# One slab of its own for the sample's transposed probabilities, and smaller slabs beside it

## The chip, the cores and the metric

The kernel runs on one core of a Trainium2 chip. The metric is the time of one execution on the device in microseconds (us), lower is better. The engines of the core are TensorE (PE; its weight loads are shown as PEld), VectorE (DVE), ScalarE (ACT), GpSimd (POOL) and SyncE (SP), which issues nearly all loads. Each runs its instructions in the order of its own list and waits for the others by semaphores.

## What is computed

One inference step of a backbone of two layers over 384 tokens of width 1024: 128 prompt tokens and 256 sample tokens with a different conditioning. Cut to what matters here:

```
mod = silu(cond) @ w_mod + b_mod                 # six vectors a layer: sh1, sc1, g1, sh2, sc2, g2
h = rms_norm(x, norm1) * (1 + sc1) + sh1
proj = h @ w_in                                  # q, k, v, latents, hyena input, gates
o_a = softmax(q_a k_a^T) v_a                     # 8 heads; the sample also reads 128 cached keys
o_b = softmax(q_b k_b^T) v_b                     # 8 heads, keys and values from a latent
o_c = hyena(hy_in)                               # two long convolutions, filters made by a small net (hy_w1, hy_w2, hy_w3)
x = x + g1 * (sum_n sigmoid(gate_n) * (o_n @ w_branch_n)) @ w_out
h = rms_norm(x, norm2) * (1 + sc2) + sh2
x = x + g2 * (silu(g) * a) @ ffn_down            # a, g = split(dwconv3(h @ ffn_up))
```

All in float32. The sample's attention has 256 queries and 384 keys for each of 16 heads a layer.

## The kernel before

Tokens lie along the free dimension, channels along the 128 partitions. A float32 product is made of three products of rounded parts, hi with hi, hi with lo, lo with hi (`mm3`, L268 to L270; most of TensorE's time). The parts are made by `hi_lo`: a ScalarE copy to the rounded type (`copy_a`, L230) and a VectorE subtraction (L234). `tt` (L237) and `stt` (L240) are VectorE's other helpers, so one line of the profile stands for many places; tiles and shapes tell them apart.

**Space.** All passing buffers come from slabs. A `Slab` is a stretch of every partition, s0 with 1920 floats and s1 to s10 with 3072, and holds one type at a time, plain or rounded float32. `Arena.alloc` looks through the slabs in order and takes, of all places that are wide enough, the one that has been free for longest (a wholly empty slab counts as 10000 steps younger, so it is taken last). When an empty slab is taken for the other type, it becomes a new tile, and its first writer waits for every reader of the old one. So which slab a buffer gets decides what its writer must wait for.

**Order.** The program is written as generators that are woven together with given ratios (`weave`), and a scheduler sorts each engine's instructions by its estimate of when each can run, with the waits that the slabs bring. A buffer at another place gives another order on all engines, not just for its own instructions.

**The places that the steps touch.** The start: identity, the tables and weights of the filter net (`filters`, L480 and on: the pieces of `hy_w3` at L498, window and bias at L500 and L501), `w_mod` in eight loads (L369), the inputs, then the first two parts of `w_in` (L248), all on SP's one queue. The filter of the first layer is made in two halves of channels by `prep` (sums and differences of weights, L237 over 128x256, and their rounded parts, 128x512 and 64x512), `taps` (matmuls L551, times the window, L237 128x512), `sizes` (absolute values on ScalarE, L569, maxima on VectorE, L237 128x256) and `spectra` (column sums L586, L588 and L589, the spread factor L594, DFT matmuls L606 and their products, L237 128x512). Beside it `mod_vec` (L372 and on) makes the modulation: matmuls L378, a ScalarE copy, transposes L302, two additions L237 over 128x16, and for the scales L240 over 128x16, which writes `avs`. `norm_h` (L413 and on) then makes `h` in eight pieces: a product (L237 128x384), two ScalarE instructions with `avs` as scale (L436), and the parts of `h` (L443 and L237, or L230 and L234). With them the first projection starts.

The attention (`attention`, L960 and on) sweeps the heads: scores, softmax, then four stages later the transposes of the probabilities (`turned`, L302) and their copies to space. For each head of the sample `sample_turn` (L1031) takes a buffer of 3x256 floats, `pTs[h]`, at the first of its two query blocks; `outputs` multiplies it with the values (L1008) and frees it, four heads at a time.

Of the kernel before, what the change touches and what calls it, by code (L numbers as in the profile page):

```python
# [38 lines left out]
PS_FFN = {"mm": "0123", "fl": "456", "tr": "456"}  # L39
N_W = 4  # L40
N_BASE = 9728
SLABS = (1920, *[3072] * 10)
R_RE = 0.25
R_F0 = 3
U_CH, U_MLA = 20, 20
# [139 lines left out]
def kernel(  # L185
# [15 lines left out]
    split_slab = Slab(ctx, tc, 2 * N_W * 1024, "split")  # L201
    h_slab = Slab(ctx, tc, 2 * KD * T, "h")
    FA = Arena([Slab(ctx, tc, n, f"s{i}") for i, n in enumerate(SLABS)])
    RA = Rounded(FA)

    def banks(**lines):
# [22 lines left out]
    def copy_a(out, in_, scale=1.0):  # L229
        act.activation(out=out, in_=in_, func=AF.Copy, scale=scale)  # L230
# [74 lines left out]
    def add_sq(k, src, first):  # L305
        if first:
            sums.append(FA.alloc(T, top=True))
        acc = sums[0].ap()
# [20 lines left out]
    def load_vecs(l):  # L329
        st = FA.alloc(4, 128)  # L330
        s = [st.ap()[:, i] for i in range(4)]

        def rows(i, r0, n, src):
            sp.dma_start(out=s[i][r0:r0 + n, :], in_=src.rearrange("(r p) -> r p", p=128))

        for r0, n, src in ((0, 2, hy_freq[l]), (2, 1, hy_b1[l:l + 1]), (3, 1, hy_b2[l:l + 1])):
            sp.dma_start(
                out=s[3][r0:r0 + n].rearrange("r (h p) -> r h p", h=2),
                in_=src.unsqueeze(1).to_broadcast([n, 2, 64]),
            )  # L340
        pv = ps_of("tr", 4)
        transpose(pv, s[3][:4])
        dve.tensor_copy(out=vecs[l][:, 112:116], in_=pv)
        yield
        rows(0, 0, 48, b_mod[l])
        rows(0, 48, 8, norm1[l])
        rows(0, 56, 8, norm2[l])
        rows(0, 64, 36, hy_short_w[l].rearrange("i n -> (i n)"))
        rows(0, 100, 12, hy_short_b[l])
        pv = ps_of("tr", 112)  # L350
        transpose(pv, s[0][:112])
        dve.tensor_copy(out=vecs[l][:, 0:112], in_=pv)
        yield
        rows(1, 0, 88, ffn_conv_w[l, 0:2].rearrange("i n -> (i n)"))
        rows(2, 0, 44, ffn_conv_w[l, 2])
        rows(2, 44, 44, ffn_conv_b[l])
        pv = ps_of("tr", 176)
        transpose(pv[:, 0:88], s[1][:88])
        transpose(pv[:, 88:176], s[2][:88])
        dve.tensor_copy(out=vecs[l][:, 116:292], in_=pv)  # L360
        st.free()
# [45 lines left out]
    def sqrt_ahead(part):  # L407

        b = FA.alloc(1)
        act.activation(out=b.ap(), in_=part, func=AF.Sqrt)  # L410
        b.free()

    def norm_h(l, which):  # L413
# [3 lines left out]
        acc = sums.pop()  # L417
        st, dg = FA.alloc(4), FA.alloc(3, 128)
        sa = st.ap()[:, 0:3]
# [43 lines left out]
    def reduce_sin(l, dst, src, fr, b, n, np_):  # L463

        a = FA.alloc(n)
        q = FA.alloc(n)
# [207 lines left out]
    def hyena_open(y):  # L674
        y.oT = [RA.alloc(4, T, top=True) for _ in range(2)]
        y.db = [RA.alloc(12, 128, top=True) for _ in range(2)]
        y.dt = [b.ap() for b in y.db]
        st = FA.alloc(12, 128)
        sp.dma_start(out=st.ap(), in_=t_dft.rearrange("p (a b) -> p a b", b=128))
        hi_lo(y.dt[0], y.dt[1], st.ap())  # L680
        st.free()
# [43 lines left out]
    def hyena_chain(y, hf):  # L725

        R, dt, tok = RA, y.dt, y.tok[hf]
        A = slice(None)
# [231 lines left out]
    def attention(heads, q_of, kp_of, ks_of, vp_of, vs_of, scale, oT, pairs=False):  # L960

        jobs = []
        pts, pTs = {}, {}
# [17 lines left out]
        def turned(pa):  # L981
            n = pa.shape[1]
            pt = ps_of("at", n, 128)
            for u in range(n):
                transpose(pt[:, u], pa[:, u])
            return pt
# [44 lines left out]
        def sample_turn(hs, i, pb):  # L1031
            for u, h in enumerate(hs):
                pt = turned(pb.ap(len(hs), 3, 128)[:, u])
                if i == 1:
                    pTs[h] = FA.alloc(3, 256)
                copy_a(pTs[h].ap()[:, :, (i - 1) * 128:i * 128], pt)
            pb.free()

# [7 lines left out]
        for j in range(j0, j1):  # L1046
            two = (2 * j, 2 * j + 1)
            for hs in (two,) if pairs else (two[:1], two[1:]):
                for i in (1, 2):
                    jobs.append((lambda hs=hs, i=i: scores(hs, i, T), lambda pb, hs=hs, i=i: sample_turn(hs, i, pb)))  # L1050
            if (j - j0) % 2:
                jobs.append((None, lambda j=j: outputs(j - 1, j == j0 + 1)))
# [10 lines left out]
    def gqa(q, proj, oT):  # L1063
        qT, kT = q["qT"], q["kT"]
        vt = [q["vc"].ap(), proj[1][1].ap(), proj[2][1].ap()]
        yield from attention(
            list(range(8)),
            lambda h: qT.ap()[:, h],
            lambda h: [b.ap()[:, h // 4, 0:128] for b in kT],
            lambda h: [b.ap()[:, h // 4, 128:512] for b in kT],  # L1070
            lambda h: proj[0][1].ap()[:, 64 * (h // 4):64 * (h // 4) + 64],
            lambda h, n: vt[n][:, 64 * (h // 4):64 * (h // 4) + 64],
            64 ** -0.5, oT, pairs=True,
        )
        for b in (qT, *kT, q["vc"], *[pr[1] for pr in proj]):
            b.free()
# [295 lines left out]
    def urgent(line, by):  # L1372

        if by < 0:
            yield from line
            return
        while True:
            with tc.high_priority(offset=by):
                if next(line, line) is line:
                    return  # L1380
            yield
# [16 lines left out]
    def chain(*lines):  # L1398
        for g in lines:
            yield from g  # L1400
# [22 lines left out]
    vl = [load_vecs(l) for l in range(NL)]  # L1423
    fl = filters(0, RA, spec, True)
    next(fl)
# [37 lines left out]
    for l in range(NL):  # L1463
# [20 lines left out]
        g_ring = Ring(FA, 8, T, top=True)  # L1484
        oA = [RA.alloc(4, T, top=True) for _ in range(2)]
        oB = []
        att = chain(prep(l, proj, q := {}, RA), gqa(q, proj, oA), urgent(mla(l, q, proj, oB, RA), U_MLA))
        gs = []
# [133 lines left out]
```

## Time and profile before

| | us |
|---|---|
| median of 3 runs | 1530.76 |
| lowest, highest | 1525.3, 1531.33 |
| the profiled execution | 1531.72 |
| its span, first to last instruction | 1529.9 |
| TensorE busy in it | 1476.9 |
| VectorE busy | 1011.2 |
| ScalarE busy | 755.0 |

The profile is of one execution. Busy time is the time in which an engine had an instruction under way; a wait is put down to what ended it. Matmuls are pipelined: the time of one stands at twice its pitch in a full stretch, and the pitch of 128x384 is what such a stretch advances by. The granted clock is TensorE's share of 2.4 GHz: 1.00 is that, 0.50 is 1.2 GHz, values between are a mean over the window. A line of the profile names the program's line that issued it, and tiles without their numbers: `s` is any of the slabs, `base` holds weights as loaded and x, `split` the parts of weights, `h` the parts of the normed input, `banks` the PSUM banks.

### The profile page before, as it was taken

The numbers are of one execution on the slowest core, as the hardware profiler recorded it, in microseconds if no ns is written. First come the engines' busy times: TensorE is split into PE (matmuls) and PEld (weight loads), VectorE is DVE, ScalarE is ACT, GpSimd is POOL, SyncE is SP. The second block draws the span as 40 slices with busy tenths as digits, with TensorE's granted clock in tenths as the row PEclk, the third lists the DMA queues.
The fourth block names the chain that finished last, engine by engine and source line by source line (L and its number), as shares of the span: only waits on it lengthen the run. The fifth ranks groups of instructions, "written<-read, shape, count | busy, mean of one in ns | idle before, by whom it ended". The sixth has DMA issues, their size and how long they took to land.

```text
span 1529.9 us, 22305 instructions
## 1 busy us (share of the span) xinstructions
PE 1476.9 (97%) x8615; PEld 1355.3 (89%) x8615; DVE 1011.2 (66%) x1938; ACT 755.0 (49%) x1380; POOL 91.3 (6%) x120
## 2 busy tenths in 40 slices
PE   5899999999999999999999999999999999999997
PEld 2588889989889799999997887999898989999997
DVE  4756658646447796677767585785564767567674
ACT  2544347555454664444546444755455455344343
POOL 0112220000000000000000121100000000000000
PEclk9789999999999999999999999999999999999999
DMA  8714453425466433344355335342243524333531
GB/s 287 225 42 132 148 187 103 143 71 159 140 216 218 160 125 109 119 154 145 104 193 166 118 129 179 99 120 78 74 130 117 193 97 138 119 116 111 166 106 60
DMA packets 182448, 210.05 MB, mean 137 GB/s; under 512 B 25940, under 2 KB 166470, under 8 KB 182342
## 3 DMA queue, kind: packets, MB, share of 16 engines
q1 hardware_dynamic: 182342, 208.63, 42.9%
q8 instruction: 68, 1.11, 0.3%
q14 instruction: 38, 0.31, 0.1%
HBM read 206.48 MB, written 2.13 MB: 136 GB/s over the span
## 4 chain that ended last, share of the span: by engine, by line
PE 85%; DMA 6%; ACT 4%; DVE 3%; issue 1%; SPq 0%; POOL 0%; DVEq 0%; ACTq 0%
PE banks L268 25%; PE banks L270 24%; PE banks L269 24%; PE banks L302 3%; DMA base<-in_w_in_dram 3%; PE banks L976 2%; PE banks L378 2%; PE banks L1008 2%; DVE s L237 1%; DVE split L234 1%; ACT s L230 1%; ACT split L230 1%; DMA base<-in_w_mod_dram 1%; DMA s<-in_hy_w_dram 1%; DVE s L234 1%
## 5 line engine op out<-in xcount | busy, mean ns | idle before, releaser
L230 ACT ACTIVATE split<-base 128x1024 fp32r<-128x1024 f32 (+2 forms) x272 | 280.8, 1041 | 354.5 <-PE banks L269 260.9
L234 DVE TENSOR_TENSOR split<-base,split 128x1024 fp32r<-128x1024 f32 (+2 forms) x272 | 327.0, 1207 | 174.2 <-ACT split L230 171.0
L268 PE MATMUL banks<-h,split 128*128 128x384 f32 x1280 | 433.6, 342 | 4.5 <-DVE h L443 2.3
L270 PE MATMUL banks<-h,split 128*128 128x384 f32 x1280 | 434.7, 340 | 1.0 <-DVE split L234 1.0
L269 PE MATMUL banks<-h,split 128*128 128x384 f32 x1280 | 434.8, 340 | 0.3 <-DVE h L234 0.3
L268 PEld LDWEIGHTS banks<-h,split 128*128 128x128 f32 x1280 | 241.4, 189 | 17.8 <-issue 8.1
L269 PEld LDWEIGHTS banks<-h,split 128*128 128x128 f32 x1280 | 242.2, 189 | 4.5 <-DVE h L234 1.5
L270 PEld LDWEIGHTS banks<-h,split 128*128 128x128 f32 x1280 | 241.9, 189 | 3.4 <-DVE split L234 1.3
L269 PE MATMUL banks<-s,split 128*128 128x384 f32 x672 | 225.4, 337 | 0.0
L270 PE MATMUL banks<-s,split 128*128 128x384 f32 x672 | 225.3, 338 | 0.0
L268 PE MATMUL banks<-s,split 128*128 128x384 f32 x672 | 222.8, 338 | 0.0
L240 DVE SCALAR_TENSOR_TENSOR s<-banks,base,s 128x127 f32<-128x127 f32 (+1 forms) x448 | 172.5, 411 | 9.6 <-ACT s L457 5.5
L230 ACT ACTIVATE s<-banks 128x384 f32<-128x384 f32 (+9 forms) x260 | 114.4, 475 | 118.6 <-PE banks L302 53.2
L230 ACT ACTIVATE s<-s 128x384 fp32r<-128x384 f32 (+4 forms) x142 | 81.6, 580 | 109.9 <-DVE s L237 48.2
L268 PEld LDWEIGHTS banks<-s,split 128*128 128x128 f32 x672 | 125.7, 188 | 3.5 <-issue 1.1
L270 PEld LDWEIGHTS banks<-s,split 128*128 128x128 f32 x672 | 126.1, 188 | 1.7 <-DVE base L240 0.8
L269 PEld LDWEIGHTS banks<-s,split 128*128 128x128 f32 x672 | 126.1, 188 | 0.9 <-issue 0.2
L237 DVE TENSOR_TENSOR s<-banks,s 128x512 f32<-128x512 f32 (+3 forms) x132 | 81.7, 645 | 43.0 <-PE banks L270 21.9
L240 DVE SCALAR_TENSOR_TENSOR base<-banks,base 128x128 f32<-128x128 f32 (+1 forms) x128 | 46.9, 412 | 78.1 <-PE banks L270 78.1
L302 PE MATMUL banks<-base,s 128*128 128x128 f32 (+1 forms) x483 | 84.1, 282 | 8.7 <-DMA s<-in_hy_short_b_dram 2.0
L302 PEld LDWEIGHTS banks<-base,s 128*128 128x128 f32 (+1 forms) x483 | 61.5, 145 | 28.9 <-issue 7.1
L234 DVE TENSOR_TENSOR s<-s,s 128x384 fp32r<-128x384 f32 (+3 forms) x102 | 66.9, 660 | 18.5 <-ACT s L230 17.6
(147 smaller groups left out, 1741.7 us busy)
## 6 DMA issues: line engine op xcount, KB each, us to landing
base<-in_w_in_dram SPq DMA_DIRECT2D x40, 1024.0 KB
base<-in_ffn_up_dram SPq DMA_DIRECT2D x40, 1024.0 KB
base<-in_w_mod_dram SPq DMA_DIRECT2D x28, 1024.0 KB
s<-in_w_mod_dram SPq DMA_DIRECT2D x14, 1024.0 KB
base<-in_ffn_down_dram SPq DMA_DIRECT2D x16, 896.0 KB
base<-in_w_branch_dram SPq DMA_DIRECT2D x24, 512.0 KB
base<-in_w_out_dram SPq DMA_DIRECT2D x8, 1024.0 KB
base<-in_ffn_down_dram SPq DMA_DIRECT2D x8, 1024.0 KB
```

The costliest lines, as they stand in the source:

```text
L230: act.activation(out=out, in_=in_, func=AF.Copy, scale=scale)
L234: dve.tensor_tensor(out=lo, in0=src, in1=f(hi), op=ALU.subtract)
L237: dve.tensor_tensor(out=out, in0=a, in1=b, op=op)
L240: dve.scalar_tensor_tensor(out=out, in0=a, scalar=s, in1=b, op0=op0, op1=op1)
L268: pe.matmul(out, l[0], r[0], start=start, stop=False)
L269: pe.matmul(out, l[0], r[1], start=False, stop=False)
L270: pe.matmul(out, l[1], r[0], start=False, stop=stop)
L302: pe.transpose(out, in_, ident[:n, :n])
L378: pe.matmul(gv[32 * j:32 * j + 32], cT[:, 2 * k + j // 2], raw[:, j // 2, (j % 2) * 512:(j % 2) * 512 + 512], start=k == 0, stop=k == KD / ...
L976: pe.matmul(out, q_of(h)[:, i * 128:(i + 1) * 128], k, start=m == 0, stop=m == len(ks) - 1)
L1008: last = pe.matmul(p[b:b + 64, u], v, pT, start=start, stop=stop, tile_position=(0, b)).ins
```

## The change

The ordinary slabs become one of 1408 and nine of 3072 floats; a slab of 3584 floats, `extra`, stands beside them. The sum per partition is 32640 floats in both. A second arena, `XA`, has the extra slab first and the same ordinary slabs behind it; only the sample's `pTs[h]` are taken from it. The extra slab has room for four of them (768 floats each), later ones go where `Arena.alloc` finds the place that has been free longest, among all slabs.

```diff
--- before.py
+++ after.py
@@ -39,7 +39,8 @@
 PS_FFN = {"mm": "0123", "fl": "456", "tr": "456"}
 N_W = 4
 N_BASE = 9728
-SLABS = (1920, *[3072] * 10)
+SLABS = (1408, *[3072] * 9)
+N_EXTRA = 3584
 R_RE = 0.25
 R_F0 = 3
 U_CH, U_MLA = 20, 20
@@ -201,6 +202,7 @@
     split_slab = Slab(ctx, tc, 2 * N_W * 1024, "split")
     h_slab = Slab(ctx, tc, 2 * KD * T, "h")
     FA = Arena([Slab(ctx, tc, n, f"s{i}") for i, n in enumerate(SLABS)])
+    XA = Arena([Slab(ctx, tc, N_EXTRA, "extra"), *FA.slabs])
     RA = Rounded(FA)
 
     def banks(**lines):
@@ -1032,7 +1034,7 @@
             for u, h in enumerate(hs):
                 pt = turned(pb.ap(len(hs), 3, 128)[:, u])
                 if i == 1:
-                    pTs[h] = FA.alloc(3, 256)
+                    pTs[h] = XA.alloc(3, 256)
                 copy_a(pTs[h].ap()[:, :, (i - 1) * 128:i * 128], pt)
             pb.free()
```

No instruction is added, removed or changed; each engine's order is another one. Lines of the kernel after stand one (from L43) or two (from L204) further down. In the rows below, `s_1_112` and the like are slab tiles, `base_101` is the tile of `base`, `split_421` or `split_420` that of the weights' parts.

On SP, at the start, behind the first `w_mod` load. Before:

```order
L369 DMA base_101<-in_w_mod_dram 128x2x1024
L498 DMA s_1_112<-in_hy_w_dram 64x2x256
L500 DMA s_1_149<-in_t_win_dram 128x3x256
L501 DMA s_1_149<-in_hy_bias_dram 128x2x256
L525 DMA s_1_149<-in_t_kdft_dram 128x1280
L334 DMA s_1_113<-in_b_mod_dram 48x128
```

and after:

```order
L371 DMA base_101<-in_w_mod_dram 128x2x1024
L500 DMA s_1_149<-in_hy_w_dram 64x2x256 x2
L502 DMA s_1_149<-in_t_win_dram 128x3x256
L500 DMA s_1_149<-in_hy_w_dram 64x2x256 x2
L503 DMA s_1_149<-in_hy_bias_dram 128x2x256
L527 DMA s_1_156<-in_t_kdft_dram 128x1280
```

The three next loads of filter weights (hy_w), which stood ten rows further down behind the inputs' loads, now stand around the window table.

On VectorE, around the first modulation, before: the rows are the copy of vectors (L360), low parts of `w_in` (L234), the norm's small matrix (L425), modulation additions (128x16), filter work (128x512, 128x256, 64x512), the norm's first products (128x384), and last `avs` (L240).

```order
L360 COPY base_101<-banks 128x176
L234 TENSOR_TENSOR split_421<-base_101,split_421 128x1024
L425 TENSOR_SCALAR s_1_268<-base_101,s_1_268 128x128 x3
L237 TENSOR_TENSOR base_101<-banks,base_101 128x16
L234 TENSOR_TENSOR split_421<-base_101,split_421 128x1024
L237 TENSOR_TENSOR s_1_143<-s_1_112,s_1_143 64x512
L237 TENSOR_TENSOR base_101<-base_101,banks 128x16
L237 TENSOR_TENSOR s_1_200<-s_1_268 128x256
L237 TENSOR_TENSOR s_1_114<-banks,s_1_200 128x512 x3
L237 TENSOR_TENSOR s_1_108<-base_101,banks 128x384 x4
L237 TENSOR_TENSOR s_1_169<-banks,s_1_169 128x512
L240 SCALAR_TENSOR_TENSOR base_101<-base_101 128x16
```

After, up to `avs` again (L242 there, L236 for the low parts, L239 for L237):

```order
L239 TENSOR_TENSOR s_1_108<-base_101,banks 128x384 x3
L239 TENSOR_TENSOR s_1_149<-s_1_124 128x256
L239 TENSOR_TENSOR s_1_108<-base_101,banks 128x384
L239 TENSOR_TENSOR s_1_149<-s_1_124 128x256
L236 TENSOR_TENSOR split_420<-base_101,split_420 128x1024 x3
L239 TENSOR_TENSOR base_101<-banks,base_101 128x16
L236 TENSOR_TENSOR split_420<-base_101,split_420 128x1024
L362 COPY base_101<-banks 128x176
L239 TENSOR_TENSOR base_101<-base_101,banks 128x16
L239 TENSOR_TENSOR s_1_114<-banks,s_1_149 128x512 x3
L239 TENSOR_TENSOR s_1_112<-banks,s_1_156 128x512
L242 SCALAR_TENSOR_TENSOR base_101<-base_101 128x16
```

All four low parts of `w_in` and the three products of the filter's DFT (s_1_114) now stand in the twelve rows that end with `avs`; above these rows stand the tap products that came behind it.

On ScalarE, between the first layer's FFN and the second layer: rounded weights (128x1024), squares for the norm (L310), the rounded copy of a DFT table (128x1536), the norm's root (L404), the copy of a modulation (128x512), and the norm (L436). Before:

```order
L230 ACTIVATE split_421<-base_101 128x1024
L310 ACTIVATE s_1_108<-base_101 128x384
L230 ACTIVATE s_4_3898<-s_7_6709 128x1536
L410 ACT_TABLE_LOAD
L410 ACTIVATE s_7_6200<-s_7_6200 128x1
L230 ACTIVATE split_421<-base_101 128x1024
L310 ACTIVATE s_1_108<-base_101 128x384
L230 ACTIVATE base_101<-banks 128x512
L404 ACTIVATE s_7_6200<-banks,base_101 128x3
L436 ACTIVATE s_1_108<-s_1_108,base_101 128x128
```

and after:

```order
L232 ACTIVATE split_420<-base_101 128x1024
L312 ACTIVATE s_3_1607<-base_101 128x384
L412 ACT_TABLE_LOAD
L412 ACTIVATE s_5_6283<-s_3_3262 128x1
L232 ACTIVATE split_420<-base_101 128x1024
L312 ACTIVATE s_3_1607<-base_101 128x384
L232 ACTIVATE base_101<-banks 128x512
L406 ACTIVATE s_3_6396<-banks,base_101 128x3
L232 ACTIVATE s_4_6704<-s_6_6225 128x1536
L438 ACTIVATE s_3_1607<-s_3_1607,base_101 128x128
```

The table's copy moved from the third row's place, in front of the weights' last copy, to behind the root.

## Rows read from the trace of the kernel before

**Rows 1.** The page, part 1: busy us, share and instructions of each engine.

```profile
PE 1476.9 (97%) x8615; PEld 1355.3 (89%) x8615; DVE 1011.2 (66%) x1938; ACT 755.0 (49%) x1380; POOL 91.3 (6%) x120
```

**Rows 2.** Windows: length, busy us (instructions) per engine, TensorE clock, DMA share, GB/s.

```profile
0.00:25.00 25.00, 10.62 (x34) 2.46 (x34) 7.71 (x17) 3.05 (x5) 0.80 (x10) 1.00 0.77 261
25.00:50.00 25.00, 19.48 (x87) 11.67 (x87) 17.27 (x35) 9.26 (x18) 2.15 (x3) 0.80 1.06 336
...
100.00:250.00 150.00, 150.00 (x877) 132.87 (x876) 99.95 (x176) 73.15 (x130) 31.28 (x39) 1.00 0.45 144
```

**Rows 3.** Chain of waits, 0 to 90 us (start, length, what); TensorE's timeline.

```profile
21.99 9.02 DMA s<-in_hy_w_dram
...
32.27 17.85 DMA base<-in_w_in_dram
...
51.27 1.89 ACT split L230 x2
...
66.53 0.61 ACT s L436 x2
...
83.93 0.67 PE L268 MATMUL banks<-h,split 128*128 128x384 f32 x1
```

**Rows 4.** Timeline of SP's loads: start, us, issuing line, tiles.

```profile
16.94 1.86 SPq L498 DMA_DIRECT2D s<-in_hy_w_dram  x3
```

**Rows 5.** Windows in front of `avs`, of the first norm, and after it.

```profile
0.00:66.50 66.50, 43.10 (x175) 23.35 (x175) 38.78 (x81) 22.60 (x40) 5.49 (x16) 0.88 0.87 279
...
66.50:83.30 16.80, 13.42 (x50) 9.30 (x50) 13.21 (x27) 13.03 (x30) 3.49 (x3) 0.70 0.22 64
...
84.00:87.00 3.00, 3.00 (x11) 3.00 (x11) 2.60 (x6) 2.53 (x6) 1.33 (x2) 0.50 0.02 5
87.00:90.00 3.00, 3.00 (x18) 3.00 (x17) 0.43 (x1) 1.71 (x5) 0.00 (x0) 0.92 0.09 26
```

**Rows 6.** VectorE in the head: timeline, then groups by form (50 to 84 us).

```profile
66.33 0.17 DVE L240 SCALAR_TENSOR_TENSOR base<-base 128x16 f32<-128x16 f32 x1
66.41 1.29 DVE L237 TENSOR_TENSOR s<-banks,s 128x512 f32<-128x512 f32 x2
...
78.76 1.89 DVE L237 TENSOR_TENSOR s<-banks,s 128x512 f32<-128x512 f32 x3 [1.81 <-ACT s L230]
80.57 2.63 DVE L234 TENSOR_TENSOR h<-s,h 128x384 fp32r<-128x384 f32 x2
83.13 1.27 DVE L237 TENSOR_TENSOR s<-banks,s 128x512 f32<-128x512 f32 x2
...
L234 DVE TENSOR_TENSOR split<-base,split 128x1024 fp32r<-128x1024 f32 x4 | 4.8, 1221 | 0.9 <-ACT split L230 0.9
...
L237 DVE TENSOR_TENSOR s<-s 128x256 f32<-128x256 f32 x8 | 3.5, 462 | 0.9 <-ACT s L569 0.9
```

**Rows 7.** Waits, 50 to 90 us: engine, for what, total, times, longest.

```profile
ACT s L436 <- DVE base L240: 6.2, 1, 6.2
```

**Rows 8.** Timelines of ScalarE, VectorE, TensorE around 821 to 834 us.

```profile
821.58 1.50 ACT L230 ACTIVATE s<-s 128x1536 fp32r<-128x1536 f32 x1
...
824.89 1.76 DVE L234 TENSOR_TENSOR s<-s,s 128x1536 fp32r<-128x1536 f32 x1 [0.31 <-ACT s L410]
...
828.06 0.66 PE L302 MATMUL banks<-base 128*128 128x128 f32 x4 [0.70 <-ACT base L230]
...
833.24 1.07 PE L378 MATMUL banks<-base 128*32 128x512 f32 x8 [1.78 <-DMA base<-in_w_mod_dram]
```

**Rows 9.** Windows in the two attentions; TensorE's waits in 333 to 353 us.

```profile
333.00:353.00 20.00, 16.85 (x95) 14.31 (x94) 8.85 (x26) 9.76 (x19) 0.30 (x2) 0.91 0.48 132
...
1080.00:1100.00 20.00, 18.29 (x112) 16.70 (x110) 12.64 (x39) 10.38 (x20) 0.30 (x2) 1.00 0.26 57
...
PE banks L302 <- DVE s L234: 2.0, 2, 1.5
```

**Rows 10.** Waits, 500 to 540 us.

```profile
PE banks L268 <- ACT h L230: 0.8, 1, 0.8
```

## The prediction, before the run

> **What bounds the kernel now.** First the busy times: TensorE works 97% of the span, and in the window from 100 to 250 us it is busy without a gap [rows 1, 2]. There a shorter wait on another engine is worth nothing; only time in which TensorE has nothing to do can be won. Second, the 25 us windows at the start: 14.4 and 5.5 us of TensorE idle in the first two [rows 2], and a granted clock of 0.80 in the second, so part of the rest is work at half speed. Third, the chain of waits of that stretch. It is a chain of loads up to 50.1 us (the filter weights land at 31.0, the first part of `w_in` at 50.1), then ScalarE's rounded copies, and from 66.53 the first norm's ScalarE instructions (L436) that make `h`, which the first projection needs; that starts at 83.9 [rows 3]. The first L436 had waited 6.2 us for the scale factors `avs`, one tiny VectorE instruction (L240, 0.17 us) in VectorE's row [rows 7]. So the head is decided by what stands in front of that instruction on VectorE. Fourth, the attention, at which the edit aims: in 333 to 353 us TensorE idles 3.15 us, in 1080 to 1100 us 1.71 us [rows 9]. That is all that better space for the probabilities could give back.
>
> **What the change does, part by part.** No instruction and no byte is added or removed; the space per partition is the same. What changes is which slab each buffer gets, hence which earlier readers a write must wait for, hence the order that the scheduler writes down.
>
> *The probabilities.* On TensorE the first attention's order between 260 and 360 us is the same row for row, and 2.0 of its 3.15 idle us are transposes that wait for VectorE's low parts (L234) [rows 9], which the extra slab doesn't move. I count 0 here, between the 4.9 us that the two idle sums would be if all of them went and an equal loss if a placement now waits for older readers; nothing in the rows leans either way, so the ends are for the range only, and I let ±2 stand for the likely part.
>
> *The head.* Before, the loads of the filter weights (`hy_w`) behind the first one went out from 16.9 us on, since their space was taken [rows 4]. In the new order three of them stand directly behind the first one, with one table between. The bytes that the one DMA queue of SP carries up to `w_in` are the same and the DMA engines are full in 25 to 50 us (share 1.06 [rows 2]), so I let `w_in` land at 50.1 as before. The effect is on VectorE: the second piece of filter work is written ahead of the four low parts of `w_in`, and so ahead of `avs`. Ahead of it come now: two tap products of the run at 66.41 (1.29), three sums over 128x256 (3 x 0.46 = 1.4), two instructions over a few columns (2 x 0.2 = 0.4, nearest to L240's 0.17), three products of 78.76 (1.89), one of the two of 83.13 (0.64): 5.6 us [rows 6]. All were behind `avs`, so they shorten what follows.
>
> Up to 66.5 us VectorE is busy 38.8 us and idle 27.7 [rows 5]. In the new order 38.8 + 5.6 = 44.4 us of work stand up to `avs`. *Bound from below:* all filter work fits into the idle time in front of `w_in`. Then ScalarE's first high part is there at 51.27 + 0.95 = 52.2 [rows 3], and VectorE does the four low parts (4.8), the three products (1.89), one more (0.64) and four small ones (0.2 each): `avs` at 60.3, 6.2 us earlier, with 16 us of idle time left in front of it. *Bound from above:* the waits stay as long as they are (27.7): `avs` at 72.1. Behind `avs` the norm took from 66.5 to the low part of the last `h` at 83.2, 16.7 us, in which VectorE was busy 13.2 and ScalarE 13.0 [rows 5, 6]; 4.9 us of that VectorE work are gone from it, though ScalarE's rows, one after the other, keep it at 14.5 at least by the 13.0. I take `avs` at 62 (1.7 behind the lower bound, because 17.3 of the 27.7 idle us lie in the first 25 us [rows 2], which is where weights that come early can be used) and 16 for the norm: `h` is whole at 78.0 instead of 83.9, at which the first projection starts. Eight L378 matmuls that stood before it stand behind its first ones now: 1.1 back, by the eight at 833.24 [rows 8]. **Head: 83.9 - 78.0 - 1.1 = 4.8 us less**, between 8.0 less (60.3 + 14.5 = 74.8) and 5.3 more (72.1 + 16 = 88.1).
>
> The clock: TensorE runs at its lower level, 1.2 GHz (0.50), in 84 to 87 us after it had idled [rows 5]; eleven matmuls of the projection fill it, where 18 fill the next 3 us: 3.0 - 11 x 0.167 = 1.2 us are lost. I leave this where it is, since the new order also lets TensorE wait for one `h` after another. The Trainium skill ("TensorE: Matmul & The Clock Gate", What's actually happening) says that the throttled state is the default and that activity releases it; the row of 84 to 87 us agrees. By it the denser filter work could keep the full clock into the projection, which would make the sum 1.2 us smaller, or the three matmuls per `h` could hold it low for longer, some 1.2 larger.
>
> *Start of the second layer (820 to 842 us).* Before, the rounded copy of a 128x1536 table stands in front of the residual work on ScalarE (1.50 at 821.58) and on VectorE (1.76 at 824.89); the split that frees the next `w_mod` buffer comes only after it, and TensorE waits 1.78 us for that load and 0.70 for ScalarE's copy [rows 8]. In the new order both are later: on ScalarE behind L404, in a gap that was idle, on VectorE behind the norm's fourth product. Up to 1.78 + 0.70 = 2.5 us go; but the 1.76 of VectorE now stands in front of the first `h`, which TensorE needs at 834.3 (833.24 + 1.07), so most of the loss can come back there. **1.0 us less**, between 2.5 less and 1.8 more.
>
> *Start of the first FFN (505 to 520 us).* ScalarE's copy of a table that lands late stands in front of an `h`, and TensorE waits 0.8 us [rows 10]; in the new order that `h` comes first. VectorE gets other work in front of its own `h` there. **0.4 less**, between 0.8 less and 0.4 more.
>
> The sum, against the profiled execution's 1531.7 us: 1531.7 - 4.8 - 1.0 - 0.4 = 1525.5. That execution stands 0.96 above the median of the runs (1530.76), so 1524.5; I say **1525.0 us**, 0.4% less.
>
> **The rivals.**
> *Slower: filter work in front of the scale factors.* VectorE takes its instructions in their order; if one of the 5.6 us moved ahead of `avs` waits (a tap matmul that stands behind a late `w_mod` load on TensorE, ScalarE's absolute value), then everything behind it waits, `w_in`'s low parts and `avs` included. For it: VectorE and ScalarE have waited for one another all through the head, and 7.7 of 25 us busy at the start show that being written early is not being done early [rows 2]. Against it: only 2.7 of the 27.7 idle us lie behind 50 us, so most of the waiting is for loads that now come earlier. It decides at 66.8 (83.9 - 1.1 - 16) for `avs`: if VectorE still idles over 22.4 us in front of it, the head is slower. With all 27.7: 1531.7 + 5.3 - 1.4 - 1 = **1534.6 us**. The Trainium skill (same page, Architectural detail, on queue depths) says that VectorE and ScalarE are strictly first in, first out; that speaks for this rival, and the 6.2 us wait for a 0.17 us instruction [rows 7] agrees.
> *The change does nothing.* Ten of the 32 buffers of transposed probabilities still find no room in the extra slab (it holds four at a time), the attention's order is the same, and the head's gain is eaten by a late ScalarE. For it: the attention's waits [rows 9] are not for the probabilities' space. Then about **1530 us**.
> *The whole gain.* Head 8.0, second layer 2.5, FFN 0.8: 1531.7 - 11.3 - 1 = **1519.4 us**. For it: the idle time in the first 25 us is three times what the moved work needs. Against it: the norm's length is ScalarE's own.
>
> **How the numbers follow.** About 0.5% (7.65 us) is what a measurement of this kernel can tell from no change: below 1523.1 counts as faster, above 1538.4 as slower. The forecast, 1521 to 1528.5, has 0.45, a third of it below 1523.1; the whole gain 0.20; nothing 0.20; slower 0.15, of which I put half past 1538.4: the second layer's attention, around 1080 to 1180 us, is written in another order too, and a loss there of twice the 1.71 [rows 9] brings the slower rival to 1538.0. So faster 0.15 + 0.20 = 0.35, slower 0.08, same 0.57. The range leaves out the outer half of the whole gain and the outer two thirds of the slower case: 1517.5 to 1534.
>
> **What would show it.** In the profile after: the first L436 at 61 to 63 us (at 72: the slower rival), the first projection matmul before 80 us; the wait of L436 for L240 gone or under 2 us; the wait for `w_mod` near 833 us gone; idle time in 333 to 353 us about 3.15 as now. Wrong would be a `w_in` that lands later than 51 us, VectorE idle over 22 us before the first L436, or a new TensorE wait of over 2 us in a stretch that is full now (a projection that waits for a slab's older readers).

## The result and the profile after

The changed kernel takes **1514.0 us** (median of 5 runs, 1512.16 to 1514.25), the kernel before 1531.33 beside it (5 runs, 1525.3 to 1532.59): ratio 0.9893, 95% interval 0.9874 to 0.9913, 1.1% less. That lies 3.5 us below the lower end of the range (1517.5). The profiled executions have spans of 1529.9 and 1512.4 us, 17.5 apart; the accounting below is made between these two.

Part 1 of the page after answers to [rows 1]: the same instructions, 11.8 us less TensorE busy time. So a large part of the gain is not idle time: the same work took less time.

```profile
PE 1465.1 (97%) x8615; PEld 1349.4 (89%) x8615; DVE 1014.3 (67%) x1938; ACT 754.8 (50%) x1380; POOL 92.8 (6%) x120
```

Where it came from shows when the start of the n-th TensorE instruction of one trace is taken from that of the other (both have 8615). The order differs a little, so it is good to about 1 us within a stage and better between full stretches:

| time in the kernel before, us | after is ahead by, us |
|---|---|
| 83 to 92 (first projection) | 16.6 to 17.3 |
| 221 | 17.3 |
| 355 (behind the first attention) | 19.3 |
| 452 to 501 | 17.0 |
| 527, in front of the first FFN's waits | 17.6 |
| 540 to 814 | 11.6 |
| 858 | 14.9 |
| 1190 to the end | 17.5 |

All of the gain is there after 83 us; the first FFN loses about 6 of it and the second layer brings as much back.

**The head.** Windows of the kernel before (first fence) and after (second; its first two rows answer to [rows 2]): length, busy us (instructions) of TensorE, its weight loads, VectorE, ScalarE, GpSimd, then the granted clock, DMA share and GB/s.

```profile
0.00:100.00 100.00, 73.22 (x303) 48.27 (x303) 61.42 (x125) 44.02 (x85) 10.71 (x21) 0.85 0.62 197
39.00:51.00 12.00, 10.32 (x48) 4.84 (x45) 7.93 (x17) 3.18 (x6) 1.18 (x2) 0.57 1.07 333
60.00:72.00 12.00, 11.07 (x39) 7.40 (x39) 11.90 (x27) 5.78 (x13) 3.25 (x3) 0.57 0.59 182
75.00:87.00 12.00, 9.34 (x30) 7.92 (x31) 8.94 (x15) 7.09 (x18) 3.50 (x3) 0.59 0.01 3
```

```profile
0.00:25.00 25.00, 8.99 (x26) 2.86 (x27) 10.51 (x23) 4.31 (x7) 0.80 (x10) 1.00 0.77 244
25.00:50.00 25.00, 23.00 (x141) 14.71 (x141) 23.16 (x48) 14.93 (x30) 6.43 (x7) 1.00 1.06 357
...
75.00:100.00 25.00, 25.00 (x147) 22.68 (x146) 16.27 (x32) 11.31 (x20) 4.34 (x5) 1.00 0.38 123
...
0.00:100.00 100.00, 79.46 (x405) 56.44 (x406) 70.98 (x144) 50.39 (x98) 15.15 (x25) 0.95 0.69 226
60.00:72.00 12.00, 11.84 (x45) 8.76 (x46) 10.10 (x22) 9.15 (x22) 3.26 (x3) 0.60 0.75 265
```

In the first 100 us TensorE issues 102 instructions more (405 for 303). Two things make room for them. It idles 20.5 us instead of 26.8, 6.2 less. And before, it worked through three stretches near its lower level, 1.2 GHz (0.57, 0.57, 0.59); there busy time times the missing clock is 10.32 x 0.43 + 11.07 x 0.43 + 9.34 x 0.41 = 13.0 us. After, only the second is left: 11.84 x 0.40 = 4.7. **By this estimate 8.3 us come from the clock**, more than from idle time; with it 14.5 of the 17.3 are named. The same instructions show it in TensorE's groups by form up to 84 us (of before, then of after): equal counts, other durations.

```profile
L551 PE MATMUL banks<-s 128*128 128x512 f32 x24 | 11.6, 641 | 3.3 <-DVE s L237 1.6 <-ACT s L230 1.6
```

```profile
L553 PE MATMUL banks<-s 128*128 128x512 f32 x24 | 8.5, 492 | 2.4 <-DVE s L239 1.2 <-ACT s L232 1.1
```

Why there is more to do early: in the chain of waits after, the second to fourth filter-weight loads go out at 6.4 to 8.3 us, and the last of them has landed at 15.5; before, they went out from 16.9 [rows 4]. (The load that lands at 31.0 in [rows 3] is a later one, of the filter's second half.) VectorE's first sums of filter weights, 128x256, start 16.0 us earlier. The chain after, then VectorE before and after:

```profile
8.31 7.18 DMA s<-in_hy_w_dram
```

```profile
28.62 0.75 DVE L237 TENSOR_TENSOR s<-s 128x256 f32<-128x256 f32 x2
```

```profile
12.58 0.76 DVE L239 TENSOR_TENSOR s<-s 128x256 f32<-128x256 f32 x2 [2.37 <-DMA s<-in_hy_w_dram]
```

Up to `avs` VectorE then has this much work (window after; the prediction counted 44.4):

```profile
0.00:61.41 61.41, 41.03 (x205) 23.61 (x206) 44.53 (x90) 26.93 (x50) 7.98 (x18) 0.98 0.84 275
```

Then the scale factors `avs` and the first projection (timelines of VectorE, ScalarE and TensorE after; brackets hold the wait before an instruction). They answer to [rows 6, 7] and to the 83.93 of [rows 3]:

```profile
61.41 1.40 DVE L242 SCALAR_TENSOR_TENSOR base<-base 128x16 f32<-128x16 f32 x1
...
76.11 0.55 DVE L236 TENSOR_TENSOR h<-s,h 128x384 fp32r<-128x384 f32 x1
...
62.85 3.62 ACT L438 ACTIVATE s<-s,base 128x128 f32<-128x128 f32 x8 [5.13 <-DVE base L242]
...
64.34 1.33 PE L270 MATMUL banks<-h,split 128*128 128x384 f32 x3 [0.16 <-DVE h L445]
65.59 1.94 PE L380 MATMUL banks<-base 128*32 128x512 f32 x8
```

The norm starts at 62.85 where it started at 66.53, and the projection at 64.34, 1.5 us behind the first L438, with the first piece of `h` for three banks. Then other work (L380, L608) fills until the next piece comes. The low part of the last piece ends at 76.66 (76.11 + 0.55): `h` is whole 12.3 us after the projection has begun.

**The first FFN.** TensorE's timeline after, then the window before and after ([rows 10] is the same place), then VectorE after:

```profile
521.09 0.66 PE L270 MATMUL banks<-h,split 128*128 128x384 f32 x1 [3.69 <-DVE s L242]
```

```profile
500.00:550.00 50.00, 48.63 (x293) 39.88 (x292) 41.04 (x91) 33.50 (x55) 0.00 (x0) 1.00 0.51 167
```

```profile
500.00:550.00 50.00, 46.31 (x248) 45.13 (x247) 40.83 (x85) 30.24 (x49) 1.59 (x1) 0.93 0.42 138
```

```profile
514.52 1.22 DVE L236 TENSOR_TENSOR split<-base,split 128x1024 fp32r<-128x1024 f32 x1 [4.98 <-ACT split L232]
```

The wait of 0.8 us for `h` is gone, but there is a new one of 3.69 us for the convolution (L242) that reads the banks, and a clock of 0.93 instead of 1.00: 46.31 x 0.07 = 3.2. VectorE had itself waited 4.98 us for the copy into `split`, whose space TensorE held: four products ran side by side, piece of `h` by piece of `h`, and so ended together.

**The second layer's start.** TensorE's timeline and a window before, then the same two views after ([rows 8]):

```profile
850.20 0.30 PE L302 MATMUL banks<-base,s 128*128 128x128 f32 x1 [0.86 <-DVE s L240]
851.89 0.58 PE L270 MATMUL banks<-h,split 128*128 128x384 f32 x1 [0.96 <-DVE split L234]
```

```profile
846.00:858.00 12.00, 10.18 (x50) 9.51 (x49) 7.49 (x15) 4.77 (x7) 0.88 (x3) 0.86 0.32 104
```

```profile
821.79 1.06 PE L380 MATMUL banks<-base 128*32 128x512 f32 x8 [2.11 <-DMA base<-in_w_mod_dram]
824.79 0.45 PE L271 MATMUL banks<-h,split 128*128 128x384 f32 x1 [1.22 <-DVE h L239]
```

```profile
834.00:846.00 12.00, 12.00 (x73) 11.16 (x71) 9.84 (x19) 6.36 (x10) 1.83 (x3) 1.00 0.29 92
```

The wait for `w_mod`, 1.78 before, is 2.11 now, and a wait for `h` of 1.22 is new. The gain comes behind them: the pauses at 850 and 852 are gone and so is their low clock (1.82 + 10.18 x 0.14 = 3.2 us). Where the 2.6 us between 858 and 1190 come from was not found. The gain belongs to no one size: counted in the same way, seven of the eight variants below with other slabs (all but experiment 9) gain 3.8 to 5.1 us between 814 and 1000 us too, where the changed kernel gains 5.4.

**The attention.** 315 to 335 us after holds the work that [rows 9] has at 333 to 353: idle 2.28 (3.15 before), with the same 2.0 us for VectorE's low parts.

```profile
315.00:335.00 20.00, 17.72 (x98) 15.42 (x99) 9.37 (x26) 9.99 (x21) 0.15 (x1) 0.91 0.49 132
```

```profile
PE banks L304 <- DVE s L236: 2.0, 2, 1.5
```

### The profile page after: what moved, and what is told of

Its sections match the earlier page's. It is cut to its first block, busy times and chain, and to the rows that moved or that the text cites. A ratio compares the mean times of both kernels' runs of the same rounds, so it can differ in the third digit from the quotient of the medians.

```text
span 1512.4 us, 22313 instructions
## 1 busy us (share of the span) xinstructions
PE 1465.1 (97%) x8615; PEld 1349.4 (89%) x8615; DVE 1014.3 (67%) x1938; ACT 754.8 (50%) x1380; POOL 92.8 (6%) x120
## 4 chain that ended last, share of the span: by engine, by line
PE 91%; DVE 3%; DMA 2%; ACT 2%; SPq 1%; issue 1%; DVEq 0%; ACTq 0%
PE banks L270 26%; PE banks L272 26%; PE banks L271 26%; PE banks L304 4%; PE banks L380 3%; PE banks L978 3%; PE banks L1010 2%; DMA base<-in_w_mod_dram 1%; DVE s L239 1%; PE banks L608 1%; PE banks L553 1%; DVE split L236 0%; PE banks L588 0%; ACT s L232 0%; DMA s<-in_hy_w_dram 0%
## 5 line engine op out<-in xcount | busy, mean ns | idle before, releaser
L236 DVE TENSOR_TENSOR split<-base,split 128x1024 fp32r<-128x1024 f32 (+2 forms) x272 | 329.1, 1216 | 175.0 <-ACT split L232 172.9
L242 DVE SCALAR_TENSOR_TENSOR s<-banks,base,s 128x127 f32<-128x127 f32 (+1 forms) x448 | 173.4, 411 | 8.2 <-ACT s L459 3.9
L232 ACT ACTIVATE s<-banks 128x384 f32<-128x384 f32 (+11 forms) x216 | 94.5, 470 | 101.5 <-PE banks L272 38.0
L232 ACT ACTIVATE s<-s 128x384 fp32r<-128x384 f32 (+3 forms) x142 | 81.7, 580 | 89.1 <-DVE s L239 47.1
L239 DVE TENSOR_TENSOR s<-banks,s 128x512 f32<-128x512 f32 (+3 forms) x132 | 81.5, 643 | 36.4 <-PE banks L272 16.2
L242 DVE SCALAR_TENSOR_TENSOR base<-banks,base 128x128 f32<-128x128 f32 (+1 forms) x128 | 46.9, 411 | 80.1 <-PE banks L272 79.9
L304 PE MATMUL banks<-base,s 128*128 128x128 f32 (+2 forms) x483 | 82.4, 274 | 6.9 <-DMA s<-in_hy_short_b_dram 4.5
L304 PEld LDWEIGHTS banks<-base,s 128*128 128x128 f32 (+2 forms) x483 | 60.6, 141 | 23.8 <-DMA s<-in_b_mod_dram 5.7
L239 DVE TENSOR_TENSOR s<-s 128x256 f32<-128x256 f32 (+4 forms) x122 | 67.1, 561 | 17.8 <-ACT s L1281 8.7
```

What stands on the lines that cost most here:

```text
L236: dve.tensor_tensor(out=lo, in0=src, in1=f(hi), op=ALU.subtract)
L239: dve.tensor_tensor(out=out, in0=a, in1=b, op=op)
L242: dve.scalar_tensor_tensor(out=out, in0=a, scalar=s, in1=b, op0=op0, op1=op1)
L304: pe.transpose(out, in_, ident[:n, :n])
```

## The experiments

Each ratio is against runs of the kernel before that were taken beside it (medians 1529.64, 1529.15 and 1529.46). "Ahead by" is counted as in the table above.

**1. The own slab without the small first one** (`own_slab_only`), from the kernel before:

```diff
-SLABS = (1920, *[3072] * 10)
+SLABS = (1920, *[3072] * 9)
+N_EXTRA = 3072
+    XA = Arena([Slab(ctx, tc, N_EXTRA, "extra"), *FA.slabs])
-                    pTs[h] = FA.alloc(3, 256)
+                    pTs[h] = XA.alloc(3, 256)
```

> The first slab stays at 1920 floats, one of the ten others becomes the slab of its own for the sample's transposed probabilities (3072 floats, four of them). In the order written for it, the filter weights' loads and the first norm stand as in the kernel before. Theory A (the gain is the smaller first slab's, through the order of the start): first projection matmul at 82 to 86 us as before, time 1528 to 1533 us. Theory B (the gain is the own slab's): 1512 to 1518 us, with the start as before and the gain in the two attentions.

Measured: 1525.43 us (8 runs), ratio 0.9972 (0.9961 to 0.9982). The window of the head is that of the kernel before:

```profile
0.00:100.00 100.00, 72.75 (x309) 48.30 (x310) 61.93 (x127) 44.07 (x85) 11.16 (x22) 0.85 0.61 198
```

The first projection starts at 82.28, as theory A says, but the time lies between the two ranges. Ahead by 1.2 us at 100 and 2.0 behind the first attention. Then 3.8 more come at the second layer's start and 1.6 go again. So the edit that the change is named for gives neither the head nor more than 0.8 us in the attention.

**2. The small first slab alone** (`small_first_only`):

```diff
-SLABS = (1920, *[3072] * 10)
+SLABS = (1408, *[3072] * 10)
```

> The first slab shrinks to 1408 floats and nothing else: ten slabs of 3072, no slab of its own. Its start is written as in the kernel after. Theory A: first projection matmul at 63 to 66 us, granted clock full up to 57 us, time 1512 to 1520 us. Theory B: 1529 to 1533 us.

Measured: 1527.4 us (10 runs), ratio 0.9989 (0.9977 to 1.0). Both expectations missed. The head is there (17.8 us ahead at 100 us, the projection from 69.31, not the 63 to 66 of theory A), but 9.3 are left at 265 us, 4.2 at 331, 0.7 at 567, and 5.1 in the end. The windows show the loss (the head first, then the two stretches behind it), with TensorE's waits in 210 to 250 us:

```profile
0.00:100.00 100.00, 78.25 (x400) 54.31 (x401) 68.37 (x143) 49.67 (x96) 14.53 (x25) 0.97 0.65 211
...
100.00:250.00 150.00, 146.21 (x826) 127.45 (x825) 91.64 (x153) 67.72 (x115) 27.20 (x35) 0.98 0.46 146
250.00:360.00 110.00, 103.31 (x637) 91.00 (x636) 69.72 (x134) 63.63 (x137) 2.12 (x5) 0.98 0.37 105
```

```profile
PE banks L268 <- ACT s L230: 1.8, 1, 1.8
PE banks L268 <- ACT s L1209: 1.0, 1, 1.0
```

The 150 us that TensorE filled before [rows 2] have 3.8 us of idle time, and VectorE does 91.6 us of work in them, where it does 100.0 in the kernel before and 109.6 in the changed one. TensorE's two longest waits in 210 to 250 are for ScalarE (its copies, L230, and the gates, L1209). That VectorE, falling behind, is what makes ScalarE late is likely but not shown.

**3. No slab kept for anyone** (`no_own_slab`): the sizes of the changed kernel, the 3584 as the last ordinary slab.

```diff
-SLABS = (1920, *[3072] * 10)
+SLABS = (1408, *[3072] * 9, 3584)
```

> All slabs in one arena: one of 1408, nine of 3072 and, as the last, one of 3584 floats that every buffer may use; no slab is kept for the probabilities. The sum per partition is that of both kernels. Theory G (the early gain comes from the small first slab, and is kept only where the long convolution and the first attention find nine ordinary slabs; with a tenth that they may use, a buffer there is written into space whose readers are late, and TensorE waits): about 15 to 17 us ahead of the kernel before at 120 us, 5 to 8 of it left at 360 us, as with the small first slab and ten of 3072; in the end 5 us faster, 1522 to 1527. Rival H (what that variant lost came from its own sizes, not from the tenth slab): the gain at 360 us is 15 us or more and the time is that of the changed kernel, 1512 to 1516.

Measured: 1524.89 us (10 runs), ratio 0.9972 (0.996 to 0.9983). 16.4 us ahead at 100 us, 8.6 at 265, 3.7 at 355, 7.6 in the end; the window of 100 to 250 us is as in experiment 2:

```profile
100.00:250.00 150.00, 146.03 (x828) 127.34 (x827) 90.46 (x152) 66.42 (x112) 27.84 (x36) 0.98 0.46 148
```

The time is that of theory G, and of the gain even less is left than the 5 to 8 us it named: with ten slabs of 3072 or more open to every buffer most of the head's gain is lost by 355 us, at both sizes of the tenth; with nine it is kept. The theory's reason, a buffer in space whose readers are late, is not shown: which buffer it is was not singled out.

**4. The probabilities last into the extra slab** (`extra_last`), from the changed kernel; 6 of 32 buffers go there, instead of 22.

```diff
-                    pTs[h] = XA.alloc(3, 256)
+                    try:
+                        pTs[h] = FA.alloc(3, 256)
+                    except MemoryError:
+                        pTs[h] = XA.alloc(3, 256)
```

> The kernel after, but the sample's transposed probabilities take the ordinary slabs first and the extra slab only where no ordinary place is left (six of 32 buffers); up to the first attention every engine's order is that of after. Theory E (the head's gain is the first slab's, and is kept because nine ordinary slabs place the first layer's long convolution well; the own slab itself is worth little): the gain at 250 us is 18 to 19 us as in after, and 1512 to 1519 us. Rival F (the own slab keeps the first attention from waiting for older readers): the gain falls by 4 us or more between 290 and 340 us, and 1518 to 1524 us.

Measured: 1512.68 us (4 runs), ratio 0.989 (0.9876 to 0.9905), as the changed kernel's 0.9893. That is theory E, and between 290 and 340 us nothing is lost (19.2 and 21.5 us ahead). So what matters about the extra slab is that the others stay out of it; its use for the probabilities is worth nothing that shows.

**5. The first projection against the order of the pieces** (`last_piece_first`), from the changed kernel: its products take the pieces of `h` from the last to the first, so none can start before `h` is whole.

```diff
-        for k in range(kk):
+        for n in range(kk):
+            k = kk - 1 - n if back else n
...
-                yield from gemm_f(p, ws[i], hT)
+                yield from gemm_f(p, ws[i], hT, back=(l, hf) == (0, 0))
```

> The kernel after, but the first six products of the first projection take the pieces of h from the last to the first, so that none can start before the last piece is there (the sum over pieces is added in another order). Theory C (part of the head's gain is that TensorE works on each piece as it comes): the first projection starts at 74 to 78 us instead of 64.3, TensorE idles 4 to 8 us before it, and the clock stays low for longer: 1519 to 1524 us. Rival (the gain is in the filter work's clock alone, the pieces don't matter): 1514 to 1516 us.

Measured: 1523.99 us (5 runs), ratio 0.9958 (0.9945 to 0.9972). TensorE's timeline (a pause of 3.44 us, and the projection at 79.83) and the window of the head:

```profile
74.96 5.22 PE L609 MATMUL banks<-s,s 128*128 128x256 f32 x12 [3.44 <-ACT s L232]
79.83 0.87 PE L270 MATMUL banks<-h,split 128*128 128x384 f32 x3
```

```profile
0.00:100.00 100.00, 75.55 (x365) 52.48 (x366) 67.81 (x139) 48.63 (x95) 13.62 (x24) 0.91 0.63 206
```

The time is that of theory C; the projection starts later than its 74 to 78, since twelve matmuls of the filter (L609) stand in front. 10.5 us ahead at 100 us instead of 17. Starting with the first piece is worth 6.5 to 7 us of the head, and the clock is part of it (0.91 for 0.95), so this and the 8.3 us above overlap. Of the 9 us between the two spans (1521.5 and 1512.4) the rest is lost behind 800 us, where the order is another one too.

**6. The first FFN bank by bank** (`ffn_bank_by_bank`), from the changed kernel: in the first group of the FFN of layer 0, pieces 4 to 7 of a product are written behind the whole product before it.

```diff
+                if wait and k >= 4:
+                    order.enter_context(tc.issue_after(held[-1]))
                 pe.matmul(out, l[0], r[0], start=k == 0, stop=False)
                 pe.matmul(out, l[0], r[1], start=False, stop=False)
+                last = pe.matmul(out, l[1], r[0], start=False, stop=k == kk - 1).ins
...
+        held.append(last)
```

> The kernel after, but in the first FFN's first four products each product's second half (pieces 4 to 7) is put behind the end of the product before, so that the first bank is finished early. Theory D (after's 3.7 us wait at 517 to 521 us and the low clock behind it come from four banks that end together): the wait falls under 1 us, the clock stays at 1.00, time 1507 to 1510 us. Rival (VectorE's own row is the limit there): the wait stays, 1513 to 1515 us.

Measured: 1510.55 us (4 runs), ratio 0.9873 (0.9853 to 0.9893). The time is half a us above the range of theory D, but in the window the wait and the low clock are gone, as it says:

```profile
500.00:550.00 50.00, 49.28 (x278) 47.73 (x279) 45.97 (x99) 34.70 (x57) 0.72 (x1) 1.00 0.48 151
```

It is 16.2 us ahead behind the FFN, where the changed kernel is 11.6. Once more, beside experiment 7:

> The variant with the hold alone once more, on the same chip as the two together: 1510 to 1512, so that the two can be told apart to half a us.

Measured: 1509.97 us (4 runs), ratio 0.9869 (0.9851 to 0.9887). It is the fastest here, 2 to 4 us ahead of the changed kernel (19.1 and 19.5 below the median of the kernel before beside it, for 17.3). The intervals overlap with the changed kernel's, so the size rests on the window.

**7. Both, 4 and 6** (`extra_last_and_bank_by_bank`):

> The two variants together: the probabilities go to the ordinary slabs first and to the extra slab only where none has room, and in the first FFN of layer 0 the last four pieces of a bank's product are issued after the whole product of the bank before. If the gains are independent of each other (theory: the hold removes the wait and the low clock at the start of the FFN, whatever the slabs' order): the time of the variant with the hold alone less 0 to 1.5 us, 1508.5 to 1511. Rival: the hold changes the order behind it, so that the two together are no better than one: 1511 to 1514. TensorE's idle time in 500 to 550 us is under 1 us by the theory.

Measured: 1516.76 us (6 runs), ratio 0.9914 (0.9898 to 0.9929): worse than either, outside both expectations. The wait that the hold removed is back, longer (timelines of TensorE and VectorE, then the same wait in experiment 4, without the hold):

```profile
520.66 0.47 PE L270 MATMUL banks<-h,split 128*128 128x384 f32 x1 [4.65 <-DVE s L242]
...
510.89 0.83 DVE L236 TENSOR_TENSOR s<-s,s 128x640 fp32r<-128x640 f32 x1 [1.82 <-ACT s L232]
```

```profile
PE banks L270 <- DVE s L242: 2.1, 2, 1.8
```

Here VectorE idles for table copies of ScalarE, this one among them, and starts the FFN's split at 513.16, 2.1 us later than the second run of the hold alone (511.07), which is about level with it up to there (17.7 and 18.2 us ahead at 501 us). So the products side by side were what made the wait in the changed kernel, but in the order of experiment 4 the hold made the wait longer (4.65 for 2.1). That it helps only where VectorE is ready to read the banks that end early fits these rows; it was not tested by itself.

**8. The transposes of x twice** (`transposes_twice`), from the kernel before: 24 short matmuls more, to see whether a fuller TensorE keeps the clock.

```diff
-            for i in range(3):
+            for i in (0, 1, 2) * 2:
```

> The kernel before, with each of the 24 transposes of the inputs (28 to 38 us) done twice into the same place: 24 more short matmuls, about 2.6 us of TensorE work where it idles; nearly nothing else moves. Theory G (the low clock of 39 to 51 us follows the idle time of 33 to 39): the granted clock of 39 to 51 us rises to 0.9 or more. If the clock alone carries the head's gain, the time falls by 3 to 5 us (1525 to 1527); if the waits behind it (57 to 60 us, for the first norm) take up what the clock gives, the time stays within 1.5 us of before (1528 to 1531).

Measured: 1526.26 us (10 runs), ratio 0.9983 (0.9968 to 0.9997). Theory G missed: in the windows the clock of the stretch that it aimed at did not change (0.57). The second stretch is lower (0.50 for 0.57), the third is at 1.00:

```profile
39.00:51.00 12.00, 9.94 (x45) 4.58 (x48) 6.67 (x15) 1.75 (x4) 0.72 (x1) 0.57 1.06 335
60.00:72.00 12.00, 10.27 (x32) 6.83 (x33) 12.00 (x26) 7.55 (x17) 3.21 (x3) 0.50 0.56 173
75.00:87.00 12.00, 10.05 (x51) 7.63 (x50) 6.68 (x14) 7.71 (x20) 3.38 (x3) 1.00 0.01 4
```

A pause is still there, now in front of 41.15 and for VectorE (TensorE's timeline):

```profile
41.15 3.64 PE L378 MATMUL banks<-split,base 128*32 128x512 f32 x16 [2.06 <-DVE base L237]
```

Busy time at the missing clock sums to 9.94 x 0.43 + 10.27 x 0.50 = 9.4 us here, for 13.0 before, and the kernel is about 3 us faster although it does more. That agrees with the clock as a cause of its own, but the order moved too and the runs spread from 1523.1 to 1532.1, so the size rests on the rows of one execution each.

**9. The gap at 57 us filled** (`gap_filled`), from experiment 6: four transposes done eight times, where TensorE pauses in front of the one stretch that is still slow.

```diff
-        for q in range(4):
+        for q in (0, 1, 2, 3) * (8 if (l, v) == (0, 1) else 1):
```

> The kernel with the first FFN's products bank by bank, and the four transposes of the first scales done eight times: 28 more short matmuls, about 3.1 us at full clock, in front of the 2.4 us in which TensorE idles at 57 to 61 us. Theory G: the clock stays at 1.00 in 60 to 71 us, 4.9 us come back, 0.7 to 2 go for the work that finds no idle time: 1506 to 1509 us. Rival (the clock falls anyway, since the transposes delay the scale factors): 1510 to 1514 us.

Measured: 1513.89 us (4 runs), ratio 0.9901 (0.9886 to 0.9917), 3 to 4 us slower than without; theory G missed. The window of it, then that of the second run of the hold alone; ScalarE at the norm's start, in the same order:

```profile
57.00:72.00 15.00, 12.02 (x68) 9.11 (x67) 13.19 (x30) 10.27 (x24) 3.26 (x3) 0.77 0.73 237
```

```profile
57.00:72.00 15.00, 12.23 (x52) 8.80 (x53) 13.10 (x28) 9.88 (x24) 3.25 (x3) 0.77 0.77 258
```

```profile
62.15 3.61 ACT L438 ACTIVATE s<-s,base 128x128 f32<-128x128 f32 x8 [4.73 <-DVE base L242]
```

```profile
62.93 3.62 ACT L438 ACTIVATE s<-s,base 128x128 f32<-128x128 f32 x8 [5.12 <-DVE base L242]
```

The repeats did nothing to the clock that shows: the kernel without them had 0.66 in 57 to 72 us in one execution (as the changed kernel has) and 0.77 in the other. By the same product (12.72 x 0.34 and 12.23 x 0.23) that stretch lost 4.3 us in one and 2.8 in the other, so such a sum from one execution is good to about 1.5 us. Nor is it the rival's reason: the scale factors were not delayed, the norm starts 0.8 us earlier. The loss lies behind the head: 17.0 us ahead at 100 us (17.3 and 18.5 without the repeats), 15.2 at 290 (18.8 and 19.9), 15.0 in the end (21.2 and 22.8). Its cause is open; the order moved there too.

## Why the prediction was right and wrong

- **The direction and the cause in the head: right.** VectorE's first filter sums start 16.0 us earlier and it does the filter work in time that was idle (10.5 and 23.2 us busy in the first two windows, for 7.7 and 17.3). Up to `avs` it does 44.5 us of work, predicted 44.4, and the first L436 (L438 now) stands at 62.85, predicted 61 to 63. One sign missed: its wait for `avs`, said to go or fall under 2 us, is 5.13 (6.2 before), as ScalarE too is done earlier. Experiments 1 to 3 show that the smaller first slab brings this, not the slab for the probabilities. "Since their space was taken" is not in [rows 4], which show only when the loads went out; how 1408 floats in place of 1920 bring the new order was not followed through the slabs.
- **"`h` is whole at 78.0 instead of 83.9, at which the first projection starts": the step that failed.** The norm started where I said and `h` was whole at 76.7, 1.3 us before I said, but the projection did not wait for it: it began at 64.34, 13.7 us ahead of the forecast's 78.0 and 1.5 us behind the norm's first instruction, and was woven with filter work. Even the forecast's best case, 8.0 us less for the head, rests on that wait. The condition "h whole" was read off the trace of before, where the projection stood behind the last low part; the order of the changed kernel was at hand and would have shown it. Experiment 5 puts that condition back: 79.83, 6.5 to 7 us of the head's 17.3 lost. The head was forecast at 4.8.
- **The clock "left where it is" (1.2 us either way): the term put far too low.** [rows 2, 5] show 0.80 and 0.70 in the head, and I priced only 84 to 87 us. All three stretches were worth 13.0 us, and by the estimate above 8.3 of them went. I had priced the idle time to a tenth of a us and not summed the busy time at low clock beside it. The Trainium skill ("TensorE: Matmul & The Clock Gate", What's actually happening) says that activity releases the throttle; I used it for one row. The trace agrees: in 75 to 87 us, where TensorE was busy 9.34 of 12 us at 0.59, it now fills the whole window of 75 to 100 at 1.00.
- **Second layer, "1.0 us less": right sign, wrong place, mis-sized.** The wait for `w_mod` did not go (2.11), and the feared wait for `h` came (1.22): together 0.7 lost (11.6 ahead at 825 us, 10.9 at 844). The gain, 3.2 us and more, is in two pauses at 850 us and the low clock there, which [rows 8] do not reach. No row here shows that the table's copy, which I named, is its cause.
- **First FFN, "0.4 less": wrong sign.** About 6 us lost, by products that run side by side; the 0.8 us wait that I priced did go. I had looked at what stands in front of `h` and not at the order of the banks behind it. This is the "new TensorE wait of over 2 us" that I named as a sign of being wrong; experiment 6 gives 4.6 back.
- **The attention, 0: right within the ±2** (2.0 us of waits as before; 2.0 us more ahead between 221 and 355 us, gone by 452; experiment 4).
- **The rivals.** "Slower" asked for VectorE idle for over 22.4 us in front of `avs`; it idled 16.9 (61.41 - 44.53). "The whole gain" (1519.4) was the nearest and still 5 us above the measured time, since it too had `h` whole and the clock as it was. "The change does nothing" is true of the part it was based on, the probabilities.
- **What stays open:** what a tenth open slab delays after 100 us, 2.8 us of the head that lie neither in idle time nor in the low clock, and what brings the second layer's gain.

## What to carry to other kernels

Sum two losses of TensorE side by side, idle time and busy time at the low clock, stretch by stretch, before pricing any edit near the start of a kernel. Where a scheduler orders the program, a change of a buffer pool is a change of order everywhere: read the new order at each place where TensorE waits, down to which piece of an operand its first matmul needs and whether the products behind it end one after another or all at once. And test the parts of such a change apart: here the part that it is named for gave nothing that shows, and two harmless-looking sizes, that of the first slab and the number of open ones, gave 1%.

## What the runs showed that was not expected

- Of a 17.3 us gain in the head, nearly half was clock by the estimate above: the same 24 matmuls of 128x512 took 641 ns each before and 492 after.
- More work made the kernel faster: 24 matmuls added to the kernel before gave 1526.26 for 1529.15 us (0.9968 to 0.9997), with 75 to 87 us at 1.00 instead of 0.59.
- Two executions of one kernel (the hold alone) had 0.66 and 0.77 of the clock in the same 15 us; a single trace does not tell a small change of clock from this.
- Two edits that each left the kernel at 1510 to 1513 us gave 1516.76 together.
